# Rotary embedding on one core: which engine adds up the products, and where the last unit's products lie

## The chip, the cores and the metric

The kernel runs on one core of a Trainium2 chip. The metric is device time in microseconds; a run is a whole execution, and the median of five runs is given. The profile is of one further execution.

## The reference

x has the shape 8 x 8 x 1024 x 64 in fp32 (16.8 MB), cos and sin are tables of 1024 x 32. Each row of 64 is cut into two halves of 32:

```
x_first, x_second = x[..., :half], x[..., half:]
out_first  = x_first * cos_cached - x_second * sin_cached
out_second = x_first * sin_cached + x_second * cos_cached
out = concatenate([out_first, out_second], axis=-1)
```

So there are four products and two sums for each pair of inputs; the output is as large as the input.

## The kernel before, in words

**Units.** x is cut into 8 units, u = 0 to 7. A unit is 128 partitions with R = 64 rows of hd = 64 numbers on each, 16 KB on a partition and 2 MB in all. All eight units lie in SBUF at once (`xt[u]`), and results are written over them. `sv[u]` is room for the second product of a unit. Units share such room: 0 with 4, 1 with 5, 3 with 6 (and 2 with 3 in this kernel). Unit 7 has a smaller one, `gt`, of K = 40 rows (lines 59 to 68). Each `w` tile holds a unit, the shared room and another unit side by side, so that one access pattern, `px[u]`, reaches both places that a product is written to.

**Transfers.** All loads and stores of x are issued by SP, in program order: the sin table, unit 0 in two halves, units 1 to 7 (lines 72 to 79), then the stores (line 143). The cos table is issued by ACT. SP waits before a store until all that writes those rows is done.

**Tables.** A matmul with the 0/1 matrix `sel` spreads sin and cos over the partitions into PSUM (`en`, `ec`, line 157); other parts of the table `tb` come from VectorE and POOL (lines 160 and 162). `plus` is the unit matrix, `minus` its negative, for TensorE's sums. POOL makes `sel` and `plus` (lines 82 to 88), ACT makes `minus`.

**Chunks.** Unit 0 is worked up by itself (lines 157 to 173). Of units 1 and 3 to 7 the rows 0-24, 24-48 and 48-64 are chunks; unit 2 has the one chunk 40-64, its other rows are done by POOL alone (`on_pool`, two products and the sums, 20 rows at a time, with `gt` as room). For each of the 19 chunks, in the order of the list `chunks`:

- ACT copies the rows from SBUF into a PSUM buffer (`stage`, line 111; two buffers take turns, and the copy for chunk c + 2 is issued after the products of chunk c),
- VectorE multiplies: `products` makes both products of all rows in one instruction (line 104 through `mul`), one into `xt[u]`, one into `sv[u]`. For unit 2, which has no `px`, it takes two instructions.
- The sums are then made by POOL (`pool_sums`, lines 107 and 108), or by TensorE in groups of 16 rows (`pe_sums`, eight matmuls into the one buffer `acc`, lines 184 and 185), which ACT copies back (`pe_back`, line 190). For the chunks in `whole`, VectorE makes products and sums itself (`alone`: two products and two sums).

Which chunk is followed by which TensorE group, copy back, POOL sum or store is written out by hand in `on_pe`, `back` and `behind`, keyed by the chunk's number. Each engine works through its own list strictly in this order.

Of the kernel before, what the change touches and what calls it, by code (L numbers as in the profile page):

```python
# [8 lines left out]
def kernel(  # L9
# [7 lines left out]
    nc = tc.nc  # L17
    fp32 = mybir.dt.float32
    TT = mybir.AluOpType
    P = nc.NUM_PARTITIONS  # L20

    b, h, seq, hd = x.shape
    half = hd // 2
    R = 64
    F = R * hd
# [3 lines left out]
    G = BK // half  # L29
    Q = 32  # L30
    H = R // 2
# [9 lines left out]
    const = ctx.enter_context(tc.tile_pool(name="const", bufs=1))  # L41
    xp = ctx.enter_context(tc.tile_pool(name="xp", bufs=1))
# [1 line left out]

    tb = const.tile([P, 2 * T], fp32, name="tb")
    tb4 = tb.rearrange("p (n t j) -> p n t j", t=2, j=half)
    ones = const.tile([P, 2 * P], fp32, name="ones")
    sel, plus = ones[0:Q, :P], ones[:, P:]
    minus = const.tile([P, P], fp32, name="minus")

    xt, sv, px = {}, {}, {}

    def both(t):

        return t.rearrange("p (w n f) -> p n w f", w=2, f=hd)

    for i, (u0, u1) in enumerate(((3, 6), (0, 4), (1, 5))):
        w = xp.tile([P, 3 * F], fp32, name=f"w{i}")  # L60
# [1 line left out]
        sv[u0] = sv[u1] = w[:, F:2 * F]  # L62
        px[u0], px[u1] = both(w[:, :2 * F]), both(w[:, F:])[:, :, ::-1]
    K = 40
    w = xp.tile([P, K * hd + F], fp32, name="w3")
    gt, xt[7] = w[:, :K * hd], w[:, K * hd:]
    sv[7], px[7] = gt, both(w[:, :2 * K * hd])[:, :, ::-1]
    xt[2], sv[2] = xp.tile([P, F], fp32, name="x2"), sv[3]


    rs, rc = sv[3][0:Q, 0:C], sv[3][0:Q, C:2 * C]
# [6 lines left out]
    for u in range(1, n_u):  # L78
        nc.sync.dma_start(out=xt[u], in_=xf[u])


    nc.gpsimd.memset(ones, 0.0)
    s3 = sel.rearrange("q (r j) -> q r j", j=Q // 2)
    nc.gpsimd.affine_select(out=s3, in_=s3, compare_op=TT.not_equal, fill=1.0,
                            base=0, pattern=[[0, 2 * P // Q], [-2, Q // 2]],
                            channel_multiplier=1)
    nc.gpsimd.affine_select(out=plus, in_=plus, compare_op=TT.not_equal, fill=1.0,
                            base=0, pattern=[[-1, P]], channel_multiplier=1)
    nc.scalar.mul(out=minus, in_=plus, mul=-1.0)

    cs, sn = tb4[:, :, 0], tb4[:, :, 1]

    def rows(t, n0, n1):
        return t[:, n0 * hd:n1 * hd].rearrange("p (n k j) -> p n k j", k=2, j=half)

    def tab(t, n0, n1):

        return t[:, n0:n1].unsqueeze(2).to_broadcast([P, n1 - n0, 2, half])

    def flat(t):  # L100
        return t.rearrange("p (n j) -> p n j", j=half)

    def mul(eng, o, a, t):
        eng.tensor_tensor(out=o, in0=a, in1=t, op=TT.mult)  # L104

    def sums(eng, o, c, s):
        eng.tensor_tensor(out=o[:, :, 0], in0=c[:, :, 0], in1=s[:, :, 1], op=TT.subtract)  # L107
        eng.tensor_tensor(out=o[:, :, 1], in0=c[:, :, 1], in1=s[:, :, 0], op=TT.add)  # L108

    def stage(pt, u, n0, n1):  # L110
        nc.scalar.copy(out=pt[:, :(n1 - n0) * hd], in_=xt[u][:, n0 * hd:n1 * hd])  # L111

    def products(pt, u, n0, n1):

        n = n1 - n0
        if u not in px:
            for o, t in ((sv[u], sn), (xt[u], cs)):
                mul(nc.vector, rows(o, n0, n1), rows(pt, 0, n), tab(t, n0, n1))
            return
        xr = pt[:, :n * hd].rearrange("p (n o f) -> p n o f", o=1, f=hd)  # L120
        tr = tb4[:, n0:n1].unsqueeze(3).to_broadcast([P, n, 2, 2, half])
        mul(nc.vector, px[u][:, n0:n1].rearrange("p n t (k j) -> p n t k j", k=2),
            xr.to_broadcast([P, n, 2, hd]).rearrange("p n t (k j) -> p n t k j", k=2), tr)

    def alone(pt, u, n0, n1):
# [4 lines left out]
        sums(nc.vector, xr, pr, sr)  # L130

    def on_pool(u, n0, n1):
        xr, gr = rows(xt[u], n0, n1), rows(gt, n0, n1)
        mul(nc.gpsimd, gr, xr, tab(sn, n0, n1))
        mul(nc.gpsimd, xr, xr, tab(cs, n0, n1))
        sums(nc.gpsimd, xr, xr, gr)

    def pool_sums(u, n0, n1):
        xr = rows(xt[u], n0, n1)
        sums(nc.gpsimd, xr, xr, rows(sv[u], n0, n1))  # L140

    def store(u, n0=0, n1=R):
        nc.sync.dma_start(out=of[u][:, n0 * hd:n1 * hd], in_=xt[u][:, n0 * hd:n1 * hd])
# [5 lines left out]
    with ExitStack() as first:  # L149
        p0, p1 = [first.enter_context(tc.tile_pool(name=n, bufs=1, space=PS))  # L150
                  for n in ("p0", "p1")]
        en = p0.tile([P, C], fp32, name="en")
        ec = [p0.tile([P, BK], fp32, name=f"ec{i}") for i in range(2)]
        pre = p1.tile([P, 4 * BK], fp32, name="pre")
        for part, r in ((en[:, :BK], rs[:, :BK]), (en[:, BK:], rs[:, BK:]),
                        (ec[0], rc[:, :BK]), (ec[1], rc[:, BK:])):
            nc.tensor.matmul(part, sel, r, start=True, stop=True)  # L157
        odd = [2 * (i % (Q // 2)) + 1 for i in range(Q)]
        for t, r in ((sn, rs), (cs, rc)):
            nc.vector.stream_shuffle(t[0:Q, H:], flat(r), odd)  # L160
        for k in range(1, P // Q):
            nc.gpsimd.tensor_copy(out=tb4[k * Q:(k + 1) * Q, H:], in_=tb4[0:Q, H:])  # L162
        mul(nc.vector, rows(sv[0], 0, H), rows(xt[0], 0, H), tab(flat(en), 0, H))
        for i in range(2):
            xr = rows(xt[0], i * G, (i + 1) * G)
            mul(nc.vector, xr, xr, tab(flat(ec[i]), 0, G))
        pool_sums(0, 0, H)
        stage(pre, 0, H, R)
        nc.scalar.copy(out=sn[:, :H], in_=flat(en))
        for i in range(2):  # L170
            nc.scalar.copy(out=cs[:, i * G:(i + 1) * G], in_=flat(ec[i]))
        products(pre, 0, H, R)
        pool_sums(0, H, R)
# [14 lines left out]
    def pe_back(u, n0):  # L188
        a = acc[u, n0].rearrange("p (k n j) -> p n k j", k=2, j=half)
        nc.scalar.copy(out=rows(xt[u], n0, n0 + G), in_=a)  # L190

    on_pool(2, 0, K // 2)


    cuts = ((0, 24), (24, 48), (48, 64))
    chunks = [(u, n0, n1) for u in (1, 3, 4, 5, 6, 7) for n0, n1 in cuts]
    chunks.insert(9, (2, K, R))
    whole = {(6, 48), (7, 24), (7, 48)}
    on_pe = {0: (1, 0), 3: (3, 0), 4: (3, 16), 6: (4, 0), 7: (4, 16), 10: (5, 0),
             11: (5, 16), 13: (6, 0)}  # L200
    back = {2: (1, 0), 4: (3, 0), 6: (3, 16), 8: (4, 0), 9: (4, 16), 11: (5, 0),
            13: (5, 16), 15: (6, 0)}
    behind = {
        2: [(pool_sums, 1, 16, 64), (store, 1)],
        5: [(pool_sums, 3, 32, 64), (on_pool, 2, K // 2, K)],
        6: [(store, 3)],
        9: [(pool_sums, 2, K, 64), (store, 2), (pool_sums, 4, 32, 64), (store, 4)],
        12: [(pool_sums, 5, 32, 64)],
        13: [(store, 5)],
        14: [(pool_sums, 6, 16, 48)],  # L210
        15: [(store, 6)],
        16: [(pool_sums, 7, 0, 24)],
        17: [(store, 7, 0, 48)],
        18: [(store, 7, 48, 64)],
    }

# [9 lines left out]
    for c, (u, n0, n1) in enumerate(chunks):  # L226
        (alone if (u, n0) in whole else products)(st[c], u, n0, n1)
        put(c + 2)
        if c in back:
            pe_back(*back[c])  # L230
        if c in on_pe:
            pe_sums(*on_pe[c])
        for f, *args in behind.get(c, ()):
            f(*args)
# [29 lines left out]
```

## Time and profile before

| | |
|---|---|
| median of 5 runs | 86.0 us (85.98 to 86.31) |
| profiled execution | 85.81 us, of which the span is 83.3 us |
| VectorE busy | 71.8 us (86%) |
| POOL busy | 65.9 us (79%) |
| PE busy | 38.7 us (46%) |
| ACT busy | 37.6 us (45%) |
| HBM read, written | 17.04 MB, 16.78 MB |

The profile divides the span into 40 slices of 2.1 us; a digit is the busy share in tenths. "Issue to landing" of a transfer runs from the start of its instruction on SP to the moment its last part is complete. A wait names the instruction whose end released it. The chain of waits is followed back from the last instruction of the span.

### The profile page before, as it was taken

Reading aid. Unit: us, or ns where it says so; the run is one execution under the profiler, and the core shown is the slowest. Engines: PE = TensorE matmul, PEld = TensorE weight load, DVE = VectorE, ACT = ScalarE, POOL = GpSimd, SP = SyncE. Lnnn points to the kernel's source line nnn. Section 1 sums busy time; section 2 is a strip of 40 time slices with the busy share of each in tenths; the row PEclk is TensorE's granted clock in tenths of the full one; section 3 lists DMA queues with packets and bytes.
Section 4 is the critical chain, followed back from the end, with each engine's and each line's share of the span. In section 5 each row is a group of like instructions: output and inputs, shape, how many; then the busy total and the mean of one; then the engine's idle time right before and its main releaser. Section 6 shows DMA issues by size and latency. Waiting matters only on the chain. (4 is left out here: it accounts for less than half of the span.)

```text
span 83.3 us, 372 instructions
## 1 busy us (share of the span) xinstructions
PE 38.7 (46%) x72; PEld 14.8 (18%) x72; DVE 71.8 (86%) x37; ACT 37.6 (45%) x33; POOL 65.9 (79%) x36
## 2 busy tenths in 40 slices
PE   0099930002994096394981968939398000000000
PEld 0043300002340041240411414224051000000000
DVE  0193999999999999999999999999999999999100
ACT  4300695462157535929368635592933664000000
POOL 5008998999999999999999999999999999600000
PEclk9999999999999999999999999999999995555555
DMA  2999999999999999999999999999999999999991
GB/s 47 256 417 460 456 385 433 440 433 448 401 440 417 441 440 425 417 417 441 440 425 433 401 433 448 433 440 425 425 417 425 456 425 448 425 417 423 425 393 65
DMA packets 2688, 33.82 MB, mean 406 GB/s; under 512 B 320, under 2 KB 320, under 8 KB 512
## 3 DMA queue, kind: packets, MB, share of 16 engines
q1 hardware_dynamic: 2640, 33.69, 95.9%
q10 hardware_dynamic: 48, 0.13, 0.5%
HBM read 17.04 MB, written 16.78 MB: 406 GB/s over the span
## 5 line engine op out<-in xcount | busy, mean ns | idle before, releaser
L104 DVE TENSOR_TENSOR w<-st,tb 128x3072 f32<-128x3072 f32 (+3 forms) x19 | 50.6, 2730 | 0.0
L111 ACT COPY st<-w 128x1536 f32<-128x1536 f32 (+1 forms) x18 | 23.4, 1302 | 21.6 <-DVE w L104 15.0
L184 PE MATMUL acc<-w,ones 128*128 128x512 f32 x32 | 18.3, 656 | 21.4 <-ACT w L190 12.3
L107 POOL TENSOR_TENSOR w<-w 128x1024 f32<-128x1024 f32 (+2 forms) x8 | 19.4, 2420 | 0.4 <-POOL tb L162 0.4
L108 POOL TENSOR_TENSOR w<-w 128x1024 f32<-128x1024 f32 (+2 forms) x8 | 19.4, 2423 | 0.0
L184 PEld LDWEIGHTS acc<-w,ones 128*128 128x128 f32 x32 | 5.9, 206 | 33.1 <-ACT w L190 18.1
L162 POOL COPY tb<-tb 32x2048 f32<-32x2048 f32 x3 | 5.7, 1885 | 5.0 <-DVE tb L160 4.9
L185 PE MATMUL acc<-w,minus 128*128 128x512 f32 x16 | 9.1, 651 | 0.0
L190 ACT COPY w<-acc 128x1024 f32<-128x1024 f32 x8 | 8.1, 1007 | 1.3 <-PE acc L185 1.3
L185 PE MATMUL acc<-w,ones 128*128 128x512 f32 x16 | 8.2, 592 | 0.0
L104 POOL TENSOR_TENSOR x<-x,tb 128x1280 f32<-128x1280 f32 x2 | 5.8, 2907 | 0.2
L104 POOL TENSOR_TENSOR w<-x,tb 128x1280 f32<-128x1280 f32 x2 | 5.8, 2914 | 0.0
L157 PE MATMUL en<-w,ones 32*128 32x512 f32 x4 | 3.7, 1089 | 4.0 <-DMA w<-in_sin_cached_dram 4.0
L107 POOL TENSOR_TENSOR x<-x,w 128x640 f32<-128x640 f32 (+1 forms) x3 | 4.9, 1626 | 0.2
L108 POOL TENSOR_TENSOR x<-x,w 128x640 f32<-128x640 f32 (+1 forms) x3 | 4.9, 1637 | 0.0
L111 ACT COPY pre<-w 128x2048 f32<-128x2048 f32 x1 | 1.9, 1870 | 6.3 <-DMA w<-in_x_dram 6.3
L104 DVE TENSOR_TENSOR w<-pre,tb 128x4096 f32<-128x4096 f32 x1 | 4.4, 4418 | 0.0
L104 DVE TENSOR_TENSOR st<-st,tb 128x1024 f32<-128x1024 f32 (+1 forms) x3 | 4.2, 1401 | 0.0
L185 PEld LDWEIGHTS acc<-w,minus 128*128 128x128 f32 x16 | 3.3, 208 | 4.4 <-issue 4.4
L185 PEld LDWEIGHTS acc<-w,ones 128*128 128x128 f32 x16 | 3.0, 190 | 3.9 <-issue 3.9
L157 PE MATMUL ec<-w,ones 32*128 32x512 f32 x4 | 3.6, 1056 | 0.0
L104 DVE TENSOR_TENSOR w<-w,en 128x2048 f32<-128x2048 f32 x1 | 2.3, 2286 | 1.4 <-PE en L157 1.4
(20 smaller groups left out, 20.3 us busy)
## 6 DMA issues: line engine op xcount, KB each, us to landing
w<-in_x_dram SPq DMA_DIRECT2D x6, 2048.0 KB, 26.9
out_dram<-w SPq DMA_DIRECT2D x6, 2048.0 KB, 12.0
w<-in_x_dram SPq DMA_DIRECT2D x2, 1024.0 KB, 6.4
x<-in_x_dram SPq DMA_DIRECT2D x1, 2048.0 KB, 16.1
out_dram<-x SPq DMA_DIRECT2D x1, 2048.0 KB, 7.8
out_dram<-w SPq DMA_DIRECT2D x1, 1536.0 KB, 7.2
out_dram<-w SPq DMA_DIRECT2D x1, 512.0 KB, 4.9
w<-in_cos_cached_dram ACTq DMA_DIRECT2D x1, 128.0 KB, 3.5
```

The costliest lines, as they stand in the source:

```text
L104: eng.tensor_tensor(out=o, in0=a, in1=t, op=TT.mult)
L107: eng.tensor_tensor(out=o[:, :, 0], in0=c[:, :, 0], in1=s[:, :, 1], op=TT.subtract)
L108: eng.tensor_tensor(out=o[:, :, 1], in0=c[:, :, 1], in1=s[:, :, 0], op=TT.add)
L111: nc.scalar.copy(out=pt[:, :(n1 - n0) * hd], in_=xt[u][:, n0 * hd:n1 * hd])
L157: nc.tensor.matmul(part, sel, r, start=True, stop=True)
L162: nc.gpsimd.tensor_copy(out=tb4[k * Q:(k + 1) * Q, H:], in_=tb4[0:Q, H:])
L184: nc.tensor.matmul(a[:, k], plus, xr[:, :, k], start=True, stop=False)
L185: nc.tensor.matmul(a[:, k], plus if k else minus, sr[:, :, 1 - k], start=False, stop=True)
L190: nc.scalar.copy(out=rows(xt[u], n0, n0 + G), in_=a)
```

## The change

Who makes the sums: `whole` keeps only the last chunk, (7, 48-64); the sums of (6, 48-64) and (7, 24-48) leave VectorE. TensorE gets nine groups instead of eight: one more each for units 1 and 6, one fewer for unit 5. POOL sums rows 32-64 of unit 1 (before 16-64), 16-64 of unit 5 (before 32-64), 32-64 of unit 6 (before 16-48), and 24-48 of unit 7 in addition.

Where products lie: the tile `w3` now holds unit 2, 48 rows of room and unit 7. The first 24 rows of the room take the second products of unit 2's chunk, and later those of rows 0-24 of unit 7. The other 24 are POOL's buffer `gt`, and later take rows 24-48 of unit 7. Unit 2 has a `px` of its own, so its chunk is one instruction. The cosine products of unit 0's first half go into this room instead of over x, and POOL's sums read them there.

Order: unit 2's chunk moves from the tenth place to the fourth, and its store ahead of unit 3's. Unit 7 is stored in three pieces (0-24, 24-48, 48-64) instead of two (0-48, 48-64).

Opening: `sel` is copied by ACT out of `plus`; POOL's second select falls away and its memset is half as wide.

```diff
-    ones = const.tile([P, 2 * P], fp32, name="ones")
-    sel, plus = ones[0:Q, :P], ones[:, P:]
+    plus = const.tile([P, P], fp32, name="plus")
+    sel = const.tile([Q, P], fp32, name="sel")
...
-    w = xp.tile([P, K * hd + F], fp32, name="w3")
-    gt, xt[7] = w[:, :K * hd], w[:, K * hd:]
-    sv[7], px[7] = gt, both(w[:, :2 * K * hd])[:, :, ::-1]
-    xt[2], sv[2] = xp.tile([P, F], fp32, name="x2"), sv[3]
+    L = R - K
+    w = xp.tile([P, 2 * F + 2 * L * hd], fp32, name="w3")
+    xt[2], xt[7] = w[:, :F], w[:, F + 2 * L * hd:]
+    sv[2], sv[7] = w[:, (R - K) * hd:(R + L) * hd], w[:, F:F + 2 * L * hd]
+    gt = w[:, F + L * hd:F + 2 * L * hd]
+    px[2] = both(w[:, K * hd:(R + L) * hd])
+    px[7] = both(w[:, F:F + 4 * L * hd])[:, :, ::-1]
...
-    nc.gpsimd.memset(ones, 0.0)
-    s3 = sel.rearrange("q (r j) -> q r j", j=Q // 2)
-    nc.gpsimd.affine_select(out=s3, in_=s3, compare_op=TT.not_equal, fill=1.0,
-                            base=0, pattern=[[0, 2 * P // Q], [-2, Q // 2]],
-                            channel_multiplier=1)
+    nc.gpsimd.memset(plus, 0.0)
...
+    nc.scalar.copy(out=sel.rearrange("q (r j) -> q r j", j=Q // 2),
+                   in_=plus[0:Q, 0:Q:2].unsqueeze(1).to_broadcast([Q, 2 * P // Q, Q // 2]))
...
-        if u not in px:
-            for o, t in ((sv[u], sn), (xt[u], cs)):
-                mul(nc.vector, rows(o, n0, n1), rows(pt, 0, n), tab(t, n0, n1))
-            return
+        m = K if u == 2 else 0
...
-            xr = rows(xt[0], i * G, (i + 1) * G)
-            mul(nc.vector, xr, xr, tab(flat(ec[i]), 0, G))
-        pool_sums(0, 0, H)
+            mul(nc.vector, rows(sv[7], i * G, (i + 1) * G), rows(xt[0], i * G, (i + 1) * G),
+                tab(flat(ec[i]), 0, G))
+        pool_sums(0, 0, H, sv[7])
...
-    chunks.insert(9, (2, K, R))
-    whole = {(6, 48), (7, 24), (7, 48)}
-    on_pe = {0: (1, 0), 3: (3, 0), 4: (3, 16), 6: (4, 0), 7: (4, 16), 10: (5, 0),
-             11: (5, 16), 13: (6, 0)}
-    back = {2: (1, 0), 4: (3, 0), 6: (3, 16), 8: (4, 0), 9: (4, 16), 11: (5, 0),
-            13: (5, 16), 15: (6, 0)}
+    chunks.insert(3, (2, K, R))
+    whole = {(7, 48)}
+    on_pe = {0: (1, 0), 2: (1, 16), 4: (3, 0), 5: (3, 16), 7: (4, 0), 8: (4, 16),
+             10: (5, 0), 13: (6, 0), 14: (6, 16)}
+    back = {2: (1, 0), 3: (1, 16), 5: (3, 0), 6: (3, 16), 8: (4, 0), 10: (4, 16),
+            12: (5, 0), 14: (6, 0), 15: (6, 16)}
     behind = {
-        2: [(pool_sums, 1, 16, 64), (store, 1)],
-        5: [(pool_sums, 3, 32, 64), (on_pool, 2, K // 2, K)],
-        6: [(store, 3)],
-        9: [(pool_sums, 2, K, 64), (store, 2), (pool_sums, 4, 32, 64), (store, 4)],
-        12: [(pool_sums, 5, 32, 64)],
-        13: [(store, 5)],
-        14: [(pool_sums, 6, 16, 48)],
-        15: [(store, 6)],
+        2: [(pool_sums, 1, 32, 64), (on_pool, 2, K // 2, K)],
+        3: [(store, 1), (pool_sums, 2, K, 64), (store, 2)],
+        6: [(pool_sums, 3, 32, 64), (store, 3)],
+        9: [(pool_sums, 4, 32, 64)],
+        10: [(store, 4)],
+        12: [(pool_sums, 5, 16, 64), (store, 5)],
+        15: [(pool_sums, 6, 32, 64), (store, 6)],
         16: [(pool_sums, 7, 0, 24)],
-        17: [(store, 7, 0, 48)],
+        17: [(store, 7, 0, 24), (pool_sums, 7, 24, 48), (store, 7, 24, 48)],
         18: [(store, 7, 48, 64)],
     }
```

More of the change, by code (lines that the diff above doesn't have):

```diff
@@ L115, in products @@
         n = n1 - n0
-        if u not in px:
-            for o, t in ((sv[u], sn), (xt[u], cs)):
-                mul(nc.vector, rows(o, n0, n1), rows(pt, 0, n), tab(t, n0, n1))
-            return
+        m = K if u == 2 else 0
         xr = pt[:, :n * hd].rearrange("p (n o f) -> p n o f", o=1, f=hd)
         tr = tb4[:, n0:n1].unsqueeze(3).to_broadcast([P, n, 2, 2, half])
-        mul(nc.vector, px[u][:, n0:n1].rearrange("p n t (k j) -> p n t k j", k=2),
+        mul(nc.vector, px[u][:, n0 - m:n1 - m].rearrange("p n t (k j) -> p n t k j", k=2),
             xr.to_broadcast([P, n, 2, hd]).rearrange("p n t (k j) -> p n t k j", k=2), tr)
@@ L132, in on_pool @@
     def on_pool(u, n0, n1):
-        xr, gr = rows(xt[u], n0, n1), rows(gt, n0, n1)
+        xr, gr = rows(xt[u], n0, n1), rows(gt, 0, n1 - n0)
         mul(nc.gpsimd, gr, xr, tab(sn, n0, n1))
@@ L136, in on_pool, with pool_sums @@
         sums(nc.gpsimd, xr, xr, gr)
-    def pool_sums(u, n0, n1):
+    def pool_sums(u, n0, n1, c=None):
         xr = rows(xt[u], n0, n1)
-        sums(nc.gpsimd, xr, xr, rows(sv[u], n0, n1))
+        sums(nc.gpsimd, xr, rows(xt[u] if c is None else c, n0, n1), rows(sv[u], n0, n1))
     def store(u, n0=0, n1=R):
```

## The prediction

> **What bounds the kernel now.** I read the page's slices first, then the transfers one by one, then what VectorE and POOL do near the end.
>
> ```profile
> span 83.3 us, 372 instructions
> ...
> DVE  0193999999999999999999999999999999999100
> ...
> POOL 5008998999999999999999999999999999600000
> ...
> DMA  2999999999999999999999999999999999999991
> ...
> q1 hardware_dynamic: 2640, 33.69, 95.9%
> ```
>
> Three rows look full: VectorE, POOL and the transfers. Only the DMA row is full from the second slice to the last but one. VectorE and POOL stop some 6 and 11 us before the span ends. A row of nines does not yet say which one binds, so I looked at the single transfers: the last load and the last six stores, each with size and time from issue to landing (the lines follow in order of time, from one narrow window each).
>
> ```profile
> w<-in_x_dram SPq DMA_DIRECT2D x1, 2048.0 KB, 36.7
> ...
> out_dram<-x SPq DMA_DIRECT2D x1, 2048.0 KB, 7.8
> ...
> out_dram<-w SPq DMA_DIRECT2D x1, 2048.0 KB, 8.1
> ...
> out_dram<-w SPq DMA_DIRECT2D x1, 2048.0 KB, 8.4
> ...
> out_dram<-w SPq DMA_DIRECT2D x1, 2048.0 KB, 8.7
> ...
> out_dram<-w SPq DMA_DIRECT2D x1, 1536.0 KB, 7.2
> ...
> out_dram<-w SPq DMA_DIRECT2D x1, 512.0 KB, 4.9
> ```
>
> With their issue times from the timeline they land so: the last load at 43.29 (issued 6.57); stores of unit 0 at 48.24 (issued 21.97), unit 1 53.02 (37.72), unit 3 57.92 (42.33), unit 2 62.70 (54.85), unit 4 67.61 (59.47), unit 5 72.47 (64.09), unit 6 77.35 (68.66), rows 0-48 of unit 7 81.01 (73.80), rows 48-64 82.24 (77.35). Whatever the issue time, full units land 4.8 to 4.9 us apart, which is 2.1 MB at 429 GB/s: they stand in one line, all loads ahead of all stores. In the packet records the 16 engines carry 80.2 us of x and table packets between 1.77 (the first) and 81.83 (the last), a stretch of 80.06: no gap at all. So **the transfers bind from end to end**, and 83.3 is 1.77 + 80.06 + 0.41 until the last landing + 1.08 of closing.
>
> The chain of waits names something else:
>
> ```profile
> 73.73 1.13 DVE w L104
> 74.86 1.15 DVE st L104
> 76.01 0.02 issue
> 76.04 0.69 DVE w L107
> 76.73 0.60 DVEq L259
> ```
>
> It follows engines, and VectorE's last sum did release the last store. But 0.5 MB is 1.2 us of traffic, and that store took 4.9 us: it stood 3.7 us behind the one before it.
>
> **What the Trainium skill says.** "DMA: Bandwidth & Descriptors", section "Where 436 GB/s comes from", puts the ceiling of the 16 ports at 435 GB/s; the trace has 429, so no schedule of the engines can speed up the stream. Its section "Queues, rings and completion order" says that on each DMA engine descriptors are consumed in ring order; the landings above agree. "SBUF — State Buffer", "Who interferes with whom", says that DMA never contends with a compute engine and that a VectorE instruction with one SBUF input does not contend with GpSimd. That fits: POOL's 128x1024 sums take 2.34 to 2.38 us wherever they stand. "TensorE: Matmul & The Clock Gate", "What's actually happening", has the clock halved after an idle window of about 3.4 us; here the first group of eight matmuls takes 5.7 us (20.28 to 25.96) and all later ones 3.7, with idle times up to 3.05 between them.
>
> **How late a store may be.** For the stream to stay full, a store's packets must be ready when those of the store ahead end. The first transfers were issued at 0.73 and moved their first packet at 1.77: 1.0 us. The last packet of the last store ended 0.41 before its landing, and the engines finish a store up to 0.4 us apart. So the limit is the landing of the store ahead less 1.9 us. Before, the tightest was unit 2: issued 54.85 against 57.92 - 1.9 = 56.0, 1.2 us in hand.
>
> **The change part by part.**
>
> Opening. POOL clears 128x128 instead of 128x256 and drops one of two selects (0.33 us). ACT makes sel with one copy. Its shape isn't in the trace; rows near it are ACT 128x128 at 0.31 and 128x512 at 0.59, so it ends between 2.8 and 3.1 (ACT is free at 2.47). TensorE needs it only when the sin rows are there, 3.94: cost 0, with 0.8 us in hand. Unit 0's two cosine products (1.22 us each) write another tile, POOL's sums (2.35) read it: same counts and shapes. In place against out of place I bound at plus or minus 0.3 us on POOL and take 0. No load moves.
>
> VectorE. Unit 2's chunk: two products of 1536 (1.75 each) become one of 3072 (3.35): -0.1. Rows 48-64 of unit 6 and 24-48 of unit 7 lose their separate sums: before, from start to start, 61.57 to 65.19 and 68.45 to 73.65, 3.6 and 5.2; as one product 2.2 and 3.3 (pitches of 16 and 24 rows). That is -1.4, -1.9: 3.4 us in all. VectorE ends at 77.3 - 3.4 = 73.9, if it never waits. Unit 2's chunk moves from tenth to fourth, its rows having landed at 18.83.
>
> POOL. Pitches from start to start: 16 rows more or less is 2.2 (6.76 for 48, 4.61 for 32), 24 rows 3.54, a 20-row block with products 8.98. From 30.86, the end of the first block, in the new order: unit 1 +4.61 = 35.5; block of unit 2 +8.98 = 44.5; rows 40-64 +3.54 = 48.0; unit 3 52.6; unit 4 57.2; unit 5 with 48 rows +6.76 = 64.0; unit 6 68.6; unit 7, rows 0-24, 72.1; rows 24-48 75.7. Before it ended at 72.15: +3.54, the new sums alone. Does it wait for VectorE? By VectorE's pitches unit 6's last chunk ends at 63.8, POOL comes at 64.0; unit 7's end at 67.1 and 70.3, POOL comes at 68.6 and 72.1. No, by 0.2 us at the tightest; a VectorE delay shifts POOL beyond that.
>
> TensorE and ACT. Group by group (3.7 each, 1.0 for the copy back, 1.44 or 1.02 for staging, in ACT's order) I find starts at 28.1, 32.9, 37.9, 42.7, 47.5, 52.3, 58.4 and 64.1, idle times of 1.1 to 2.3. The wait to watch is ACT's for TensorE in a copy back, for the next staging copy queues behind it and VectorE behind that: the tightest is unit 4's third chunk, staged at 43.7, wanted at 44.1. The last group ends 67.9, its copy back 68.9, and staging for the last chunk 69.9, wanted at 70.3. No stall.
>
> Stores: issue, limit, margin in hand.
> - unit 2: 48.0, 51.1, 3.1
> - unit 3: 52.6, 56.0, 3.4
> - unit 4: 57.3, 60.8, 3.5
> - unit 5: 64.0, 65.7, 1.7
> - unit 6: 68.9 (ACT's copy is last), 70.6, 1.7
> - unit 7, rows 0-24: 72.2, 75.4, 3.2
> - rows 24-48 (the store ahead lands at 79.18): 75.7, 77.3, 1.6
> - rows 48-64: behind that on SP, 76.1, limit 79.1, 3.0
>
> SP is in order, so a store that waits for POOL holds up only later stores, all wanted later. The new third piece costs 0.33 us of SP, hidden. Every margin is above the 1.2 us with which the stream ran full before. The order of units 2 and 3 changes nothing in bytes.
>
> What remains is the split itself. Packets of 16, 12 and 4 KB took 611, 460 and 159 ns: 8 ns each beside the bytes. Rows of 12 KB become two of 6 KB: 8 rows per engine at 8 ns, and one more completion packet of 9 ns: **+0.07 us**, at the very end of the stream. From both sides: 0, and 0.2 if a short packet of 6 KB fares as badly against its bytes as 4 KB did.
>
> Sum: 85.81 of the profiled run + 0.07 = 85.88; the median shown stands 0.19 above that run, so 86.0 + 0.07 = **86.07 us**.
>
> **Rivals.** *Faster: VectorE's end sets the time*, as the chain of waits has it. The last store then goes out at 76.1 instead of 77.35, 1.25 us sooner: 84.8. Against it stands the 3.7 us that this store already queues. Chance 0.04.
>
> *Slower: the stream runs dry at unit 6 because TensorE's last group is late.* It has one group more, and its copy back now stands last ahead of a store. Place: the store of unit 6; point: a copy back ended after 70.6, so a last group over 5.4 us. At the cold rate, 5.7, it is 0.3 us late: 86.4. Were every group cold from the second on, ACT, staging and VectorE fall behind cumulatively: by the same queue sums VectorE ends at 87.0, the last store is 7.9 us behind its limit of 79.1, and the time is near 94. For it: the clock does fall to half at the end of this trace. Against it: only after TensorE's work is over, and the idle times now are shorter than the 3.05 it survived. Chance 0.09, including POOL late by more than 1.6 us, which ends alike.
>
> *Not what it says:* VectorE waits for staging anyway and keeps none of its 3.4 us. The time is still 86.07, as long as the margins hold; it is inside the forecast.
>
> **Numbers.** A measurement of this kernel can tell about 0.3% (0.26 us) from no change. Margins hold: 0.87, at 86.0 to 86.3 with the split's bounds and the scatter of the runs (85.98 to 86.31). Faster 0.04, slower 0.09. The range 85.8 (the profiled run) to 86.4 takes in the small end of the slower rival.
>
> **What would show it.** DMA row still nines to the last but one slice; packets without a gap; full stores 4.9 us apart, and landings of unit 7 near 79.2, 81.0 and 82.3; VectorE ending near 74 and POOL near 75.7; the last store taking some 6 us to land. Wrong, if there is a gap in the DMA row near 64 to 78, if a matmul group after the first takes over 4 us, or if the last landing moves by over 0.3 us.

## The result, and the profile after

The changed kernel takes 85.43 us (median of 28 runs) against 86.02 of the kernel before (47 runs): ratio 0.994, 95% interval 0.9926 to 0.9953. That is 0.6% **faster**, below the forecast range of 85.8 to 86.4.

First the page of the changed kernel, the same rows as before:

```profile
span 83.5 us, 386 instructions
...
DVE  0193999999999999999999999999999999940000
...
POOL 3009989999999999999999999999999999991000
...
DMA  1999999999999999999899898999999898999990
...
q1 hardware_dynamic: 2784, 33.69, 95.8%
```

The span is not shorter: 83.5 against 83.3. VectorE ends two slices sooner, POOL two later. The eights in the DMA row are no gap: between the first packet's start (1.75) and the last one's end (82.01) the packets take 80.37 us for each of the 16 engines, in a stretch of 80.27. The stream is as full as it was. Now the stores of unit 2 and of units 3 to 6, then the three pieces of unit 7, in order of time, each with size and time from issue to landing:

```profile
out_dram<-w SPq DMA_DIRECT2D x1, 2048.0 KB, 10.1
out_dram<-w SPq DMA_DIRECT2D x1, 2048.0 KB, 10.4
out_dram<-w SPq DMA_DIRECT2D x1, 2048.0 KB, 10.7
out_dram<-w SPq DMA_DIRECT2D x1, 2048.0 KB, 8.8
out_dram<-w SPq DMA_DIRECT2D x1, 2048.0 KB, 8.2
out_dram<-w SPq DMA_DIRECT2D x1, 768.0 KB, 7.4
out_dram<-w SPq DMA_DIRECT2D x1, 768.0 KB, 5.8
out_dram<-w SPq DMA_DIRECT2D x1, 512.0 KB, 6.6
```

They are issued at 47.83, 52.44, 57.05, 63.83, 69.35, 71.95, 75.45 and 75.87, and land up to 82.48 (before: 82.24). Each takes longer from issue to landing than its bytes alone need, which is 4.9 us for a full unit, 1.8 and 1.2 for the pieces: each still stands in line. So inside the span nothing was gained.

The gain is **outside the span**. The profiled execution of the kernel before took 85.81 us with a span of 83.32: 2.49 us lie around it. Of the changed kernel it took 85.42 with 83.50: 1.92. In 27 executions of the changed kernel this rest is 1.87 to 1.97; in 57 of the kernel before, timed in the first batch of experiments, 2.28 to 2.60, median 2.46, with the same median span of 83.5. Between these medians the rest is 0.53 us shorter (2.46 to 1.93); the whole difference of the times is 0.59.

The transfers can be asked for behind the end of the span too. Kernel before, 83.4 to 87 us (packets, then their queues: packets, MB, share of the engines' time):

```profile
DMA packets 1, 0.01 MB, mean 2 GB/s; under 512 B 0, under 2 KB 0, under 8 KB 0
## 3 DMA queue, kind: packets, MB, share of 16 engines
q14 instruction: 1, 0.01, 0.9%
```

The same stretch of the changed kernel:

```profile
DMA packets 0, 0.00 MB, mean 0 GB/s; under 512 B 0, under 2 KB 0, under 8 KB 0
## 3 DMA queue, kind: packets, MB, share of 16 engines
issues: line engine op xcount, KB each, median us to landing
```

Before, one packet of kind "instruction" (8 KB, 85.54 to 86.05 by the packet records) comes 2.2 us behind the last instruction of the program. After, there is none. That packet is no part of the kernel's data; by its kind it brings instructions to an engine. In the records all packets of this kind stand under queue 14 (q14), and for which engine one is they do not say.

### The profile page after: what moved, and what is told of

Read it like the earlier page. It is cut to its first block, busy times and chain, and to the rows that moved or that the text cites. A ratio compares the mean times of both kernels' runs of the same rounds, so it can differ in the third digit from the quotient of the medians.

```text
span 83.5 us, 386 instructions
## 1 busy us (share of the span) xinstructions
PE 43.8 (52%) x80; PEld 16.8 (20%) x80; DVE 68.5 (82%) x30; ACT 38.8 (47%) x35; POOL 69.0 (83%) x37
## 4 chain that ended last, share of the span: by engine, by line
POOL 66%; issue 10%; PE 5%; DMA 4%; DVE 3%; POOLq 2%
POOL w L110 26%; POOL w L109 24%; POOL w L106 14%; PE en L156 5%; DMA w<-in_sin_cached_dram 4%; DVE w L106 3%; POOL tb L161 2%; POOLq L257 2%; POOLq L109 0%; POOLq L106 0%
## 5 line engine op out<-in xcount | busy, mean ns | idle before, releaser
L106 DVE TENSOR_TENSOR w<-st,tb 128x3072 f32<-128x3072 f32 (+2 forms) x19 | 54.7, 2956 | 0.2 <-ACT st L113 0.2
L183 PE MATMUL acc<-w,plus 128*128 128x512 f32 x36 | 21.2, 674 | 20.5 <-ACT w L189 11.6
L109 POOL TENSOR_TENSOR w<-w 128x1024 f32<-128x1024 f32 (+3 forms) x11 | 23.7, 2156 | 0.2
L110 POOL TENSOR_TENSOR w<-w 128x1024 f32<-128x1024 f32 (+3 forms) x11 | 23.7, 2153 | 0.0
L183 PEld LDWEIGHTS acc<-w,plus 128*128 128x128 f32 x36 | 6.9, 213 | 33.8 <-ACT w L189 18.2
L106 POOL TENSOR_TENSOR w<-w,tb 128x1280 f32<-128x1280 f32 x4 | 11.6, 2908 | 0.2
L184 PE MATMUL acc<-w,plus 128*128 128x512 f32 x18 | 9.2, 592 | 0.0
L156 PE MATMUL en<-w,sel 32*128 32x512 f32 x4 | 3.7, 1089 | 3.9 <-DMA w<-in_sin_cached_dram 3.9
L184 PEld LDWEIGHTS acc<-w,plus 128*128 128x128 f32 x18 | 3.4, 190 | 4.3 <-issue 4.3
L156 PE MATMUL ec<-w,sel 32*128 32x512 f32 x4 | 3.6, 1056 | 0.0
L109 POOL TENSOR_TENSOR w<-w,w 128x1024 f32<-128x1024 f32 x1 | 2.3, 2333 | 0.3 <-POOL tb L161 0.3
L159 DVE STREAM_SHUFFLE tb<-w 32x1024 f32<-32x1024 f32 x2 | 2.5, 1278 | 0.0
L106 DVE TENSOR_TENSOR w<-w,ec 128x1024 f32<-128x1024 f32 x2 | 2.4, 1218 | 0.0
```

Of the source, the lines that this page charges most:

```text
L183: nc.tensor.matmul(a[:, k], plus, xr[:, :, k], start=True, stop=False)
L184: nc.tensor.matmul(a[:, k], plus if k else minus, sr[:, :, 1 - k], start=False, stop=True)
```

## The experiments

The first theory was that some engine's **list of instructions** has another length, and that this moves the fetch out of the closing. By the trace (busy instructions and those on the sequencer), VectorE's list went from 56 to 50 entries, TensorE's and SP's grew (four more matmul calls; three more on SP), ACT's and POOL's kept their number. The rival was that the relief of VectorE, or the smaller pieces, moves the end.

### Which engine's list

**One more TensorE group on the kernel before:**

```diff
-             11: (5, 16), 13: (6, 0)}
+             11: (5, 16), 13: (6, 0), 16: (6, 0)}
```

> The kernel before, with TensorE's last group issued a second time behind its own copy back (four calls, 16 entries of the profile more, read by nobody). The gain of the change lies outside the span: 85.81 less 83.3 is 2.5 us before, 85.42 less 83.5 is 1.9 after, and the trace of before has one packet of kind instruction, 8 KB, 2.2 us behind the span, which after lacks. Theory PE (the longer list of TensorE moves this fetch out of the closing): 85.4, 1.9 us outside the span, no late packet. Theories DVE and SP (the shorter list of VectorE, or the longer one of SP): 86.0 and 2.5. Theory work (the gain comes from what the engines do, no list's length matters): 86.0.

Measured: 86.04 us, ratio to before 0.9991 (0.9967 to 1.0014), 2.46 us outside, packet 2.20 us behind the span. TensorE's list does not matter here.

**Six idle instructions on VectorE of the changed kernel:**

```diff
...
+    for i in range(6):
+        nc.vector.memset(pad[:, i:i + 1], 0.0)
```

(`pad` is a small tile of its own that nothing else uses; here and below the line that makes it is left out.)

> The changed kernel with six memsets of one column on VectorE at its end, in time that VectorE has idle (some 0.1 us each, from 74 us on), so that VectorE's list is as long as before. Theory DVE: 86.0, 2.5 us outside the span, the late packet is back. Theories PE, SP and work: 85.4 and 1.9.

Measured: 85.98, ratio 0.9993 (0.9977 to 1.001), 2.47 outside, the span unchanged at 83.5. Six instructions of a tenth of a microsecond, in idle time, take back the whole gain. Behind the span:

```profile
DMA packets 1, 0.01 MB, mean 2 GB/s; under 512 B 0, under 2 KB 0, under 8 KB 0
## 3 DMA queue, kind: packets, MB, share of 16 engines
q14 instruction: 1, 0.01, 0.7%
```

The fetch is back, 2.20 us behind the span. All other parts of the change are still in this kernel: together they are worth nothing that this measurement can see.

**Three pieces on the kernel before, two on the changed one:**

```diff
-        17: [(store, 7, 0, 48)],
+        17: [(store, 7, 0, 24), (store, 7, 24, 48)],
```

> The kernel before with unit 7 stored in three pieces (0-24, 24-48, 48-64), its sums as before. Theory SP (the longer list of SP, or the pieces): 85.4 and 1.9 us outside. Theories PE and DVE: 86.05 and 2.5: the split itself costs 0.07.

Measured: 86.1, ratio 0.9995 (0.9972 to 1.0018), 2.45 outside.

```diff
-        17: [(store, 7, 0, 24), (pool_sums, 7, 24, 48), (store, 7, 24, 48)],
+        17: [(pool_sums, 7, 24, 48), (store, 7, 0, 48)],
```

> The changed kernel with unit 7 stored in two pieces as before (0-48, 48-64). Theory SP: 86.0 and 2.5 us outside. Theories PE and DVE: 85.35 and 1.9, the split's 0.07 saved.

Measured: 85.47, ratio 0.9946 (0.9925 to 0.9967), 1.92 outside, no packet. The pieces, and SP's list, are not the cause. The split's own cost is too small to show in either.

### Length or late work, and where the step is

**The six memsets at VectorE's start** (the lines of the second experiment, ahead of everything):

> The changed kernel with the same six memsets on VectorE at its start, where VectorE waits for the sin rows until 3.8 us anyway. Theory length (the number of entries in VectorE's list, wherever they stand): 86.0, 2.5 us outside the span, the late packet. Theory late work (what VectorE still does after 74 us holds up the closing): 85.4 and 1.9.

Measured: 85.99, ratio 0.9997 (0.9984 to 1.0009), 2.49 outside, packet 2.22 behind the span. So it is the length, not what VectorE does late.

**Two and four memsets at the end:**

> The changed kernel with two memsets on VectorE at its end: 52 entries in its list, against 50 in the changed kernel and 56 before. Theory length: a step, either 85.4 with 1.9 us outside or 86.0 with 2.5, nothing between. Theory late work: 85.4 plus a part of the 0.6, about 85.6.

> The changed kernel with four memsets on VectorE at its end, 54 entries. Theory length: the other side of the step, or the same, nothing between 85.4 and 86.0. Theory late work: about 85.8.

Measured: two, 85.51, ratio 0.9938 (0.9916 to 0.996), 1.92 outside, no packet. Four, 85.95, ratio 1.0007 (0.9988 to 1.0026), 2.38 outside, packet. It is a step, between 52 and 54 entries.

**Unit 6's part of the change alone, on the kernel before:**

```diff
-    whole = {(6, 48), (7, 24), (7, 48)}
+    whole = {(7, 24), (7, 48)}
...
-        14: [(pool_sums, 6, 16, 48)],
-        15: [(store, 6)],
+        15: [(pool_sums, 6, 32, 64), (store, 6)],
```

(`on_pe` and `back` get the group (6, 16) as in the changed kernel.)

> One part of the change alone on the kernel before: unit 6's last chunk is made by products, its sums by TensorE (rows 16-32) and POOL (32-64); unit 7, the rooms, the opening and the stores as before. VectorE's list falls from 56 to 53 entries, its work by 1.4 us. Theory length: 85.4 if the step lies above 53, else 86.0; and the same side as the two-memset and four-memset kernels say. Theory work (relief of VectorE moves the end): 85.7, a share of 1.4 in 3.4 of the 0.6. The stream stays full in both.

Measured: 85.54, ratio 0.995 (0.9934 to 0.9966), 1.91 outside, no packet: nearly all of the gain, with 53 entries.

**The same with one memset of one column on VectorE:**

> The kernel with unit 6's part of the change alone (53 entries on VectorE, 85.54), and one memset of one column on VectorE at its end: 54 entries. Theory length: 86.0, 2.5 us outside the span, the late packet. Theory work: 85.55.

Measured: 86.02, ratio 1.0006 (0.9984 to 1.0029), 2.45 outside, packet 2.21 behind the span. One tiny instruction costs half a microsecond. The step lies **between 53 and 54 entries**; the theory that relief of VectorE's work pays falls.

### Is it VectorE's alone, and does it stay

**More instructions on ACT and on POOL of the changed kernel.** Eight, and then sixteen, copies of one column on ACT; one memset on POOL; one memset on POOL beside six on VectorE.

> The changed kernel with eight copies of one column on ACT at its end, when ACT is idle: 59 entries in ACT's list instead of 51. If the step at 54 holds for ACT's list as it does for VectorE's: 86.0 and the late packet. If each engine's list has its own place, and this one's is not near: 85.4.

Measured: 85.67 us (ratio 0.9958, 0.9932 to 0.9984); the rest is 1.87 to 1.97 in ten executions and 2.29 to 2.50 in eight. A mixture; the profiled one was of the first sort, without a packet. (By the records ACT's list goes from 49 to 57 entries here and to 65 with sixteen; the expectations have two too many.)

> The changed kernel with sixteen copies of one column on ACT at its end instead of eight; with eight, about half the executions had 1.9 us outside the span and half 2.4. If ACT's list has a place of its own near 59 entries: at 67 all executions have 2.4 or more outside, 86.0. If the eight copies only disturbed some executions: a mixture again, or 85.4.

Measured: 85.7 (0.9969, 0.9954 to 0.9984), and my expectation failed: the rest is 1.88 to 1.97 in all executions. A packet is there, 0.30 us behind the span instead of 2.2, and it costs nothing outside; the median span is 0.3 us longer.

> The changed kernel with one memset of one column on POOL at its end (POOL's list one entry longer than in both kernels). In the run with one product of 512 elements on POOL a late packet came back with 2.1 us outside the span instead of 1.9. If it is the length of POOL's list that did it: 85.6, 2.1 us outside, the late packet. If it was the later end of POOL: 85.4 and 1.9.

Measured: 85.62 (0.996, 0.9935 to 0.9986), 2.05 outside, packet 1.85 behind the span. POOL's list has a place too, just above its present length, and it costs about 0.12 us.

> The changed kernel with six memsets on VectorE and one on POOL. If the closings of the engines run side by side and the slowest counts: 86.0, 2.5 us outside. If they follow one another: 86.15, 2.65. Either way two late packets.

Measured: 85.71 (0.9974, 0.994 to 1.0008), 2.17 to 2.26 outside, one packet in the records, 1.84 us behind the span. Neither expectation holds: with POOL's instruction added, VectorE's six cost less (0.26 us) than without it.

**Twelve and twenty-four memsets at the start of the kernel before.** If the fetch belongs to a place in the list, a still longer list should bring it forward into the span.

```diff
...
+    for i in range(12):
+        nc.vector.memset(pad[:, i:i + 1], 0.0)
```

> The kernel before with twelve memsets of one column on VectorE at its start, where it waits for the sin rows: 68 entries in its list instead of 56, no other difference. Theory place: the fetch is set off at a fixed place of the list and costs what of it is not over when the engine needs it, so a still longer list sets it off earlier; the late packet comes less than 2.2 us behind the span, and less than the 0.55 is paid: 85.4 to 85.9, outside 1.9 to 2.4. Theory step (a list over 53 entries pays 0.55): 86.0 and 2.5.

> The same with twenty-four memsets, 80 entries. Theory place: the packet lies inside the span, or ahead of its end, and nothing is paid: 85.45, outside 1.9; the kernel before becomes as quick as the changed one by doing more. Theory step: 86.0 and 2.5.

Measured: twelve, 85.77, ratio 0.9962 (0.9932 to 0.9993), 1.94 outside. Twenty-four, 85.74, ratio 0.9979 (0.9964 to 0.9994), 1.95 outside. The late packet is gone from behind the span. For twelve it is here, in the stretch 71.4 to 72.0:

```profile
DMA packets 19, 0.25 MB, mean 423 GB/s; under 512 B 3, under 2 KB 3, under 8 KB 3
## 3 DMA queue, kind: packets, MB, share of 16 engines
q1 hardware_dynamic: 18, 0.25, 99.3%
q14 instruction: 1, 0.01, 3.2%
```

For twenty-four it lies at 61.85. By the records VectorE has begun 58 of its 68 entries when the packet starts in the first, and 61 of its 80 in the second: with twelve more, nearly the same place counted from the start of the list. The kernel before gets quicker by doing more, as the theory of a place says; a fixed step would have given 86.0. About 0.2 us of it is lost again inside the span, whose median is 83.8 in both, against 83.6 of the kernel before in the same batch. I have no explanation for that.

> The changed kernel with twelve memsets on POOL at its end, of 0.1 us each, ahead of nothing. Theory place: the packet is earlier than the 1.85 us behind the span that one memset gives (four more instructions gave 1.5 in the run with four products), outside 1.9 to 2.1, 85.4 to 85.6. Theory step: 85.6 and 2.1.

Measured: 85.43, ratio 0.9946 (0.9916 to 0.9976), packet at 80.56, inside the span, 1.77 outside. Same direction.

### Is the cover as large as the prediction said

The other half of the prediction, that the stores had slack, was tested by making one late:

```diff
...
+    def idle():
+        mul(nc.gpsimd, pad, tb[:, :512], tb[:, 512:1024])
...
-        17: [(store, 7, 0, 24), (pool_sums, 7, 24, 48), (store, 7, 24, 48)],
+        17: [(store, 7, 0, 24), (idle,), (pool_sums, 7, 24, 48), (store, 7, 24, 48)],
```

> The changed kernel with one more product of 512 elements on POOL (1.2 us by the 128x1280 rows at 2.91) ahead of the sums of unit 7's rows 24-48; its result is not used. Their store goes out 1.2 us later, near 76.65, under the limit of 77.3 of the prediction: theory cover, 85.4. Theory POOL's end binds (it stands last in the chain of waits of the changed kernel): 86.6.

Measured: 85.68 (0.9959, 0.9937 to 0.998). The store goes out at 76.66 and the last landing is at 82.51, as without it (82.48): the delay is hidden. Of the 0.25 us more than the changed kernel takes, 0.16 lie outside the span (2.09 against 1.93), with a packet 1.83 behind it, as with one memset on POOL.

> The same with four such products, 4.8 us: the store of rows 24-48 goes out near 80.2, 2.9 us over the limit of 77.3. Theory cover: the stream runs dry for 2.9 us, 88.3. Theory POOL's end binds: 90.2.

Measured: 88.38 (ratio 1.0257, 1.0204 to 1.0309). The columns are each engine's busy time, the clock, the DMA share and GB/s in three stretches:

```profile
74.00:78.50 4.50, 0.00 (x0) 0.00 (x0) 0.11 (x1) 0.00 (x0) 4.34 (x4) 0.50 0.96 405
78.50:81.50 3.00, 0.00 (x0) 0.00 (x0) 0.00 (x0) 0.00 (x0) 2.17 (x2) 0.50 0.01 4
81.50:85.30 3.80, 0.00 (x0) 0.00 (x0) 0.00 (x0) 0.00 (x0) 0.00 (x0) 0.50 0.86 345
```

In the same stretch the changed kernel has

```profile
78.50:81.50 3.00, 0.00 (x0) 0.00 (x0) 0.00 (x0) 0.00 (x0) 0.00 (x0) 0.50 1.02 421
```

The stream is dry for 2.7 us (78.82 to 81.53 by the packet records) while POOL works. The store goes out at 80.70 and lands at 83.99 instead of 81.23, 2.76 late, so the true limit was 80.70 - 2.76 = 77.94; the prediction had put it at 77.3. From this store's issue to its first packet pass 0.83 us, and the last packet of the store ahead ends 0.48 before its landing (79.30): together 1.3, where the prediction allowed 1.9.

## Why the prediction was wrong

**The step that failed is the last line of the sum**, "85.81 of the profiled run + 0.07". It carries the time around the span over unchanged, as a constant that was never looked at. The prediction counted 1.08 us of closing inside the span, and not the 2.49 between span and device time. That is where the gain arose: 1.92 in place of 2.49, 0.57 us less in the profiled executions. The late packet stood in the trace of before; the queues were read only up to the last landing. None of the rivals named it either: the faster one went through VectorE's last store, which is refuted, since that store goes out 1.5 us sooner and lands no sooner.

**The sums inside the span held.** VectorE ends at 73.98 (worked out 73.9) and POOL at 75.42 (75.7). The stores of units 2 to 5 leave within 0.3 us of the list; so do those of unit 7. Packets of 6 KB take 234 ns where 460 was the time for 12 KB: 8 ns for each split, as worked out. The prediction's mechanism, a stream that binds and covers the engines, passed the strongest test, the store made late: 88.3 was expected and 88.38 came. That the two agree to 0.1 us is luck in part, for the store went out 0.5 us later than expected, the limit lay 0.6 later, and 0.2 came from behind the span. The delay of 2.76 us in the span is what shows the mechanism. A change that took 3.4 us of work off VectorE is worth nothing by it.

**One step inside the span failed too, hidden by its margin.** The prediction held TensorE's clock safe because the idle times would be shorter than the 3.05 us survived before. They were, and still unit 6's first group, the last but one of all, ran slow at its start:

```profile
58.23 2.05 PE L183 MATMUL acc<-w,plus 128*128 128x512 f32 x2 [2.44 <-ACT w L189]
60.07 1.64 PE L184 MATMUL acc<-w,minus 128*128 128x512 f32 x2
61.54 1.02 PE L183 MATMUL acc<-w,plus 128*128 128x512 f32 x2
62.40 1.02 PE L184 MATMUL acc<-w,plus 128*128 128x512 f32 x2
```

It took 5.2 us instead of 3.7, and a group of over 4 us was one of the prediction's own signs of being wrong. ACT's copy back and the staging behind it came later, VectorE waited 0.17 us for its last chunk, and unit 6's store left at 69.35 instead of 68.9. The limit of 70.6 hid it: this rival came halfway.

The argument itself was unsound, for the length of an idle time doesn't decide. The kernel with six memsets on VectorE at its end has the same TensorE work and the same idle time, and stays fast:

```profile
58.16 1.10 PE L184 MATMUL acc<-w,plus 128*128 128x512 f32 x2 [2.43 <-ACT w L190]
```

In the traces the granted clock changes only in steps of 3.41 us (full from 23.75 to 57.88, ten steps, then half to 61.30 in the changed kernel). Over all 20 traces, 256 such steps began at full clock. After every one with 2.0 us or more without a matmul the clock was halved; after none with 1.95 or less; with 1.96 or 1.97 it was halved in five cases of six. Of the 2.44 us here, 2.09 fell into one step; of the 2.43 with the six memsets, whose steps lie elsewhere, at most 1.6; of the 3.05 before, at most 1.8. Where the steps lie differs from trace to trace (the first full one begins at 23.5 to 26.7 us), so it was luck that the 3.05 did no harm.

**What is shown, and what stays open.** Shown: the gain follows the length of VectorE's list, with a step between 53 and 54 entries. With 54 to 56 entries the late packet is there 2.2 us behind the span and the rest is 2.4 to 2.5; below, and with 68 or 80, it isn't there and the rest is 1.9. (This holds where no other engine's list was lengthened, TensorE's and SP's aside.)

The packet's times say more. In the seven profiled executions with 54 to 56 entries and POOL's list as it was, the packet starts 2.20 to 2.23 us behind the span and takes 0.38 to 0.57, and the device time, counted from the start of the span, ends 0.23 to 0.24 us ahead of the packet's end in every one. So the measured time moves with the end of this packet (the constant fits, if device time and span do not begin at the same moment; the records don't say where the device time begins). With POOL's one memset, and with its one product, the packet starts 1.85 and 1.83 us behind the span, and the offset is the same 0.23: POOL's place costs less because its packet comes some 0.37 us sooner. With sixteen copies on ACT the packet has ended 0.83 us behind the span, within the 1.92 that pass without any packet, and costs nothing outside.

The Trainium skill, "Runtime: NRT & Kernel Launch", section "Instruction fetch mechanics", says that each engine streams its instructions by its own DMA queue in blocks, and that crossing a boundary is "mostly hidden". The runs agree that a fetch within the program is nearly hidden, and differ on the closing: there it costs 0.5 us. That VectorE stands still for its block in the closing is the reading that fits; no view shows an engine's instructions behind the span, so it is argued. Open: why eight copies on ACT give two sorts of executions; why POOL's memset lowers the cost of VectorE's six, with one packet in the records where two were expected; and why four products on POOL leave 2.13 us outside though their packet ends sooner than with one, and twelve memsets only 1.77.

## What to carry to other kernels

Split the measured time into the span and the rest, and look at both before saying that a change is hidden: here the DMA stream was full from end to end, which made the inside proof against the change, and the difference of 0.6% came from behind the last instruction. When a small gain or loss doesn't show in the span, look for a packet of kind "instruction" behind its end, and repeat with a few idle instructions on the engine whose list changed: that tells the length of a list from the work. A margin in a full stream can be measured by making a transfer late on purpose, once inside the margin and once beyond it.

## What the runs showed of the hardware that I had not expected

An engine's list that is one instruction longer (53 to 54 on VectorE) can cost 0.5 us, and twelve more can give half of it back. The time between span and device time is no constant of the chip: 1.78 to 2.54 us in the profiled executions of these kernels. In nine of the eleven that have a packet of kind "instruction" 1.4 us or more behind the span, the measured time keeps a fixed distance of 0.23 to 0.24 us to that packet's end. TensorE's clock was halved for 3.41 us after a step of 3.41 us with 2.09 us of idle time in it, while an idle time of 3.05 that was cut by the border of two steps was harmless. A store issued 1.4 us ahead of the landing of the store before it (79.30 less 77.94) would still have kept the stream full.
